# SBUF offsets of matmul operands, and 128-row score passes, in a four-layer trunk kernel

## The chip, the cores and the metric

The kernel runs on one core of one Trainium2 chip. The metric is the device time of one execution in microseconds (us); lower is better. TensorE (PE) does the matmuls, VectorE (DVE), ScalarE (ACT) and GpSimd (POOL) the element-wise work, and DMA queues issued from SyncE (SP) load the weights.

## The reference

A diffusion trunk of four layers over 512 latent tokens and 256 context tokens of 1024 channels. Layer i has a token mixer (0 and 3: gated short convolution; 1: windowed attention with sinks; 2: differential attention) and a gated convolutional FFN of width 2816. All arithmetic is float32.

```python
h = h + gt1 * y                                    # y: the mixer's output
a, g = jnp.split(x @ w_up, 2, axis=-1)             # conv_ffn
return (jax.nn.silu(dwconv(g, conv_w) + conv_b) * a) @ w_down
# layer 1: 16 query heads, 4 KV heads of 64 channels, blocks of 128 query rows
s_lat = jnp.einsum("bqhgd,bkhd->bhgqk", q_j, k_j) * scale    # neighbouring blocks
s_lat = jnp.where(mask, s_lat, -jnp.inf)
s_ctx = jnp.einsum("bqhgd,bkhd->bhgqk", q_j, kc) * scale     # all 256 context keys
p = jax.nn.softmax(jnp.concatenate([s_lat, s_ctx, s_sink], axis=-1), axis=-1)
```

## The kernel before

Float32 accuracy comes from split operands: every value is a high part and a low part in a reduced float32 (fp32r), and a product is three passes, high·high, low·high and high·low (`mm3`, lines 158 to 162; `tok_project`, lines 675 to 677, has its own copy). A weight block arrives by DMA as `wr`, ACT rounds it to `wh` (L108), DVE subtracts to get `wl` (L109). A pass streams a moving operand of 256 or 512 columns against a stationary block of 128 by 128.

Program order: layer 0 convolution (tiles pb, pc, ph, down projection pd), FFN (up projections pg and pa, down projection pd over pairs of its 22 chunks of 128 channels), then layer 1 (`window_gqa`), its FFN, layer 2 (`diff_attn`), its FFN, layer 3. Up projections have normalised activations `xh`, `xl` moving and weights stationary; pd has the mixer's product `mh`, `ml` moving. The first passes of a phase (tile pre) do both halves of a chunk pair. The latent stream is 512 columns wide, or two halves of 256 where phases overlap; the context stream is 256 wide.

Layer 1 first projects tokens (tile pj: K and V, then two groups of queries, each over 6 token tiles and 8 chunks), with weights moving and tokens stationary. `post_kv` normalises and rotates K, splits it into high `ks` (stored twice side by side, 128 rows after the transpose) and low `kl` (64 rows per head, two heads in a tile), transposes both on TensorE (tile pkt) and copies them to `kT1` and `kT2`. `pre` splits four query heads into `qs`, in which high and low part of a head lie side by side, and transposes (tile pqt) to `qT` of 128 rows. A score `psS` of one query head and 128 queries is then three passes for context queries and six or seven for latent ones (`scores`): a two-column pass that writes the sink logit (L789), the latent keys against `kT1` (L792), the masks of the edge blocks (L795), the context keys against `kT1` (L796), and the two low passes against `kT2` (L797 context, L799 latent), which use only the 64 rows of the query's high part. DVE takes the maximum (L801), ACT the exponential (L803), POOL scales by the reciprocal sum (L812). `values` transposes the probabilities (pPT, L828), ACT and DVE split them (L831, L832), and TensorE multiplies with V (pO, L838); the sums go to `m`, `mh`, `ml`, the operands of the out projection, in a rotating set of buffers (L817).

What sets the order: the code makes generators (`scores`, `values`, `prefetch`, down projections as filler), `timeline` interleaves them by a list of due times, and the framework's scheduler then orders each engine's queue, waiting by semaphores where tiles depend on each other or share memory. Tiles come from pools: a pool hands out addresses in the order of its `tile` calls, a tag rotates over `bufs` buffers, and a pool that is opened after another has closed takes over its memory and waits for its readers. So the place of a `tile` call decides the byte offset of that tile and of all behind it.

Of the kernel before, what the change touches and what calls it, by code (L numbers as in the profile page):

```python
# [45 lines left out]
class Trunk:  # L46
# [133 lines left out]
    def setup(self, es):  # L180
        tc, nc, A = self.tc, self.nc, self.A
        self.cp = cp = es.enter_context(tc.tile_pool(name="const", bufs=1))
        self.pp = es.enter_context(tc.tile_pool(name="psum", bufs=1, space=PSUM))
        self.WR, self.WS = 3, 5
        self.wpool = es.enter_context(tc.tile_pool(name="w", bufs=1))
        es.enter_context(tc.tile_pool(name="top", bufs=1, side="right")).tile([P, 8], F32, name="top")

        npk = self.A["pack"].shape[1]
        pk = cp.tile([P, -(-npk // 16) * 16], F32, name="pack")
        nc.sync.dma_start(pk[:, :npk], self.A["pack"])  # L190
        pos = 0
# [12 lines left out]
        nc.scalar.activation(self.cpair, craw, AF.Silu)  # L204
        eye = self.ntmp("eye")[:, :P]
        make_identity(nc, eye)
        self.identr = cp.tile([P, P], F32R, name="identr")
        nc.vector.tensor_copy(self.identr, eye)
        self.ident = self.identr.bitcast(F32)
        self.ones = cp.tile([P, P], F32, name="ones")  # L210
        nc.gpsimd.memset(self.ones, 1.0)
        self.mhalf = cp.tile([P, 16], F32, name="mhalf")
        nc.gpsimd.memset(self.mhalf, -0.5)

        self.ada_b = [take(6, KC) for _ in range(DEPTH)]
        self.g1 = [take(KC) for _ in range(DEPTH)]
        self.g2 = [take(KC) for _ in range(DEPTH)]
        self.fcw = [take(NF, 3) for _ in range(DEPTH)]
        self.fcb = [take(NF) for _ in range(DEPTH)]
        self.scw = {l: take(KC, 3) for l in (0, 3)}  # L220
        self.sink = take(16)
        self.subln = take(1)
        self.mods = {}
        for l in range(DEPTH):
            for s in ((0, 1) if l < 3 else (0,)):
                self.mods[l, s] = cp.tile([P, 6, KC], F32, name=f"mod{l}_{s}")
        hL = [cp.tile([P, SEQ], F32, name=f"hL{k}") for k in range(KC)]
# [14 lines left out]
    def ada_first(self):  # L242

        nc = self.nc
        for j in range(KC):
# [14 lines left out]
            cols = acc[:, 2 * P:].rearrange("p (m v e) -> p m v e", m=2, v=2)[:, :, :, 0]  # L260
            md = self.cp.tile([P, 2, 2], F32, name=f"md{j}", tag="md", bufs=KC)
            nc.vector.tensor_tensor(md, cols, self.ada_b[0][:, 0:2, j:j + 1].to_broadcast([P, 2, 2]), ALU.add)
            gs = self.cp.tile([P, 2], F32, name=f"gs{j}", tag="gs", bufs=KC)
            nc.vector.scalar_tensor_tensor(gs, md[:, 1, :], 1.0, self.g1[0][:, j:j + 1].to_broadcast([P, 2]),
# [234 lines left out]
    def pads(self, y, streams):  # L499
        self.gp = []  # L500
        for i in range(2):
            g = y.tile([P, TOK + 16], F32, name=f"gp{i}")
            for col in (0, SEQ + 1, TOK + 2):
                self.nc.gpsimd.memset(g[:, col:col + 1], 0.0)
            self.gp.append(g)
# [175 lines left out]
    def window_gqa(self, xn):  # L681
# [4 lines left out]
        self.PT, self.rl = 3, 0  # L686
        ytc = self.tc.tile_pool(name="yt1", bufs=1, side=self.yside)
        yt = ytc.__enter__()
        tabs = {which: self.rope_table(1, which, yt) for which in "kq"}
        sink = self.sink  # L690
        sel = y.tile([P, P], F32R, name="sel")
        sinkx = y.tile([P, 32], F32R, name="sinkx")
        pick = self.ntmp("pick")
        nc.gpsimd.memset(pick, 0.0)
        nc.gpsimd.memset(pick[0:1, :P], 1.0)
        nc.gpsimd.memset(pick[32:33, :P], 1.0)
        nc.vector.tensor_copy(sel, pick[:, :P])
        nc.vector.tensor_copy(sinkx, pick[:, P:P + 32])
        nc.vector.tensor_copy(sinkx[0:1, :16], sink[0:1])
        sinkh = self.ntmp("sinkh", F32R)[:, :16]  # L700
        nc.vector.tensor_copy(sinkh, sink)
        nc.vector.tensor_tensor(sinkx[32:33, :16], sink[32:33], sinkh[32:33].bitcast(F32), ALU.subtract)
        identr = self.identr
# [3 lines left out]
        kT1 = {0: y.tile([P, 4, SEQ], F32R, name="kT1L"), 1: y.tile([P, 4, CTX], F32R, name="kT1C")}  # L707
        kT2 = {0: y.tile([P, 2, SEQ], F32R, name="kT2L"), 1: y.tile([P, 2, CTX], F32R, name="kT2C")}
        vs = [y.tile([P, 4, 2, HD], F32R, name=f"v{t}") for t in range(NT)]
        qraw = [y.tile([P, D], F32, name=f"qraw{t}") for t in range(NT)]  # L710

# [3 lines left out]
        def post_kv(tt, ps):  # L715
# [5 lines left out]
            ks = yt.tile([P, 4, 2, HD], F32R, name="ks", tag="pt", bufs=self.PT)  # L721
            kl = yt.tile([P, 512], F32R, name="kl", tag="pt", bufs=self.PT)[:, :256]
            k3 = kr.rearrange("p (h d) -> p h d", d=HD)
            nc.scalar.copy(ks, k3[:, :, None, :].to_broadcast([P, 4, 2, HD]))
            nc.vector.tensor_tensor(kl.rearrange("p (h d) -> p h d", d=HD), k3, ks[:, :, 0, :].bitcast(F32), ALU.subtract)
            pt = self.ps("pkt")
            for j in range(4):
                self.tr(pt[:, j * P:(j + 1) * P], ks[:, j].rearrange("p a d -> p (a d)"))
            for j in range(2):
                self.tr(pt[:, 512 + j * P:512 + (j + 1) * P], kl[:, j * P:(j + 1) * P])  # L730
            sid, o = (0, tt * P) if tt < SEQ // P else (1, tt * P - SEQ)
            nc.scalar.copy(kT1[sid][:, :, o:o + P], pt[:, 0:512].rearrange("p (j t) -> p j t", j=4))
            nc.scalar.copy(kT2[sid][:, :, o:o + P], pt[:, 512:768].rearrange("p (j t) -> p j t", j=2))

        self.wlimit = self.wpos + 12 if PRM['pf1'] else self.wlimit
        tts = [4, 5, 0, 1, 2, 3]
        self.tok_project([A["l1_wa_qkv"][2, kp] for kp in range(4)], xn, tts, post_kv)
        for grp in range(2):
            def post_q(tt, ps, grp=grp):
                self.qk_post(ps, 8, tabs["q"], rope_tt(tt), qraw[tt][:, grp * 512:(grp + 1) * 512], yt)  # L740
            self.tok_project([A["l1_wa_qkv"][grp, kp] for kp in range(4)], xn, tts, post_q)
# [10 lines left out]
        mask = xb.tile([P, 2, P], F32R, name="mask")  # L752
        nc.vector.tensor_copy(mask, maskf)

        def pre(j, tt):
# [18 lines left out]
        def scores(u):  # L774
            _, _, tt, j, _, _ = units[u]
            qT = qTs.pop(u)
            plist = pls[u] = []
            hs = slice((j % 2) * HD, (j % 2) * HD + HD)
            keys, b0, nl = keys_of(tt)
# [5 lines left out]
            for i in range(4):  # L785
# [97 lines left out]
        for _ in self.rest:  # L883
            pass
        self.close_x()
        yc.__exit__(None, None, None)
        self.xside = self.yside
# [10 lines left out]
    def diff_attn(self, xn):  # L898
# [7 lines left out]
        vsp = dr.__enter__().tile([2, 8, P, NT, P], F32R, name="vspill")  # L906
        nlam = y.tile([P, 16], F32, name="nlam")[:, :1]
        kT = [y.tile([P, 8, TOK], F32R, name=f"kT{grp}") for grp in range(2)]
# [137 lines left out]
        def finish(st):  # L1046
# [258 lines left out]
```

## Time and profile before

| what | value |
|---|---|
| median of 3 runs | 3202.27 us (3201.17 to 3203.89) |
| the profiled execution, its own time | 3210.95 us |
| span of its trace | 3209.1 us |
| mean granted TensorE clock | 0.981 |
| PE busy (share of span) | 3136.9 us (98%) |
| PE weight loads | 2717.5 us (85%) |
| DVE busy | 2177.0 us (68%) |
| ACT busy | 1126.4 us (35%) |
| POOL busy | 698.7 us (22%) |
| DMA moved | 322.66 MB, mean 101 GB/s |

Busy time is the union of an engine's records. A matmul's record is modelled at its end and reaches into the next one, so the busy share of PE says little; the start times of successive records are what can be compared. [...] The profiled execution is 0.27% above the median of the runs.

### The profile page before, as it was taken

The numbers are of one execution on the slowest core, as the hardware profiler recorded it, in microseconds if no ns is written. First come the engines' busy times: TensorE is split into PE (matmuls) and PEld (weight loads), VectorE is DVE, ScalarE is ACT, GpSimd is POOL, SyncE is SP. The second block draws the span as 40 slices with busy tenths as digits, with TensorE's granted clock in tenths as the row PEclk, the third lists the DMA queues.
The fourth block names the chain that finished last, engine by engine and source line by source line (L and its number), as shares of the span: only waits on it lengthen the run. The fifth ranks groups of instructions, "written<-read, shape, count | busy, mean of one in ns | idle before, by whom it ended". The sixth has DMA issues, their size and how long they took to land.

```text
span 3209.1 us, 44079 instructions
## 1 busy us (share of the span) xinstructions
PE 3136.9 (98%) x17548; PEld 2717.5 (85%) x17548; DVE 2177.0 (68%) x3138; ACT 1126.4 (35%) x1864; POOL 698.7 (22%) x581
## 2 busy tenths in 40 slices
PE   8999999999998999999999999989999999999999
PEld 7889888888987788888888888778888888898888
DVE  5775887786575566677666576478788766565555
ACT  4212322222243566422222244277532333242222
POOL 2222221231134333122000033277211110010000
PEclk9999999999998799899999999999999999999999
DMA  6431434332111000233333212421255522222322
GB/s 227 145 119 53 138 126 144 132 119 99 47 62 34 20 1 27 87 115 104 128 109 130 78 48 70 135 73 57 91 196 164 200 98 99 99 86 88 104 91 79
DMA packets 105198, 322.66 MB, mean 101 GB/s; under 512 B 12576, under 2 KB 27552, under 8 KB 104992
## 3 DMA queue, kind: packets, MB, share of 16 engines
q1 hardware_dynamic: 100512, 313.26, 28.6%
q0 software_dynamic: 4480, 6.58, 1.1%
q8 instruction: 138, 2.26, 0.3%
q14 instruction: 68, 0.56, 0.1%
HBM read 311.26 MB, written 8.53 MB: 100 GB/s over the span
## 4 chain that ended last, share of the span: by engine, by line
PE 90%; DVE 5%; ACT 2%; issue 1%; DMA 1%; POOL 1%; SPq 0%; DVEq 0%; ACTq 0%; POOLq 0%
PE pd L160 9%; PE pd L161 9%; PE pd L162 9%; PE pg L160 6%; PE pg L162 6%; PE pg L161 6%; PE pa L160 6%; PE pa L161 6%; PE pa L162 6%; PE pj L675 3%; PE pj L676 3%; PE pj L677 3%; PE pO L838 2%; PE pPT L828 1%; PE pre L161 1%; PE pre L162 1%
## 5 line engine op out<-in xcount | busy, mean ns | idle before, releaser
L108 ACT CAST wh<-wr 128x1024 fp32r<-128x1024 f32 x380 | 392.9, 1049 | 1211.2 <-PE pd L161 357.2
L109 DVE TENSOR_TENSOR wl<-wr,wh 128x1024 fp32r<-128x1024 f32 x380 | 485.5, 1291 | 175.5 <-ACT wh L108 173.3
L160 PE MATMUL pd<-mh,wh 128*128 128x256 f32 (+1 forms) x1712 | 566.3, 331 | 10.7 <-DVE hC L435 10.2
L161 PE MATMUL pd<-ml,wh 128*128 128x256 f32 (+1 forms) x1712 | 562.0, 328 | 0.3 <-DVE ml L1069 0.3
L162 PE MATMUL pd<-mh,wl 128*128 128x256 f32 (+1 forms) x1712 | 562.2, 328 | 0.0
L435 DVE SCALAR_TENSOR_TENSOR hL<-pd,mod,hL 128x512 f32<-128x512 f32 (+1 forms) x512 | 333.9, 659 | 257.7 <-PE pd L162 257.1
L294 POOL PARTITION_ALL_REDUCE acc<-acc x34 | 222.8, 6584 | 1103.7 <-DVE acc L292 1103.7
L160 PEld LDWEIGHTS pd<-mh,wh 128*128 128x128 f32 x1712 | 324.5, 190 | 44.0 <-DVE hC L435 10.6
L160 PE MATMUL pg<-xh,wh 128*128 128x256 f32 (+1 forms) x992 | 352.3, 355 | 1.5 <-ACT gp L580 1.5
L162 PE MATMUL pg<-xh,wl 128*128 128x256 f32 (+1 forms) x992 | 352.1, 355 | 0.0
L161 PE MATMUL pg<-xl,wh 128*128 128x256 f32 (+1 forms) x992 | 351.9, 355 | 0.0
L161 PE MATMUL pa<-xl,wh 128*128 128x256 f32 (+1 forms) x992 | 351.5, 354 | 0.0
L160 PE MATMUL pa<-xh,wh 128*128 128x256 f32 (+1 forms) x992 | 351.4, 354 | 0.0
L162 PE MATMUL pa<-xh,wl 128*128 128x256 f32 (+1 forms) x992 | 351.0, 354 | 0.0
L161 PEld LDWEIGHTS pd<-ml,wh 128*128 128x128 f32 x1712 | 324.4, 190 | 31.1 <-DVE ml L1069 0.5
L162 PEld LDWEIGHTS pd<-mh,wl 128*128 128x128 f32 x1712 | 324.8, 190 | 30.5
L292 DVE SCALAR_TENSOR_TENSOR acc<-adaw,csilu,acc 128x1024 f32<-128x1024 f32 x238 | 300.9, 1293 | 57.7 <-DMA adaw<-l_ada_w 56.9
L160 PEld LDWEIGHTS pg<-xh,wh 128*128 128x128 f32 x992 | 187.5, 189 | 28.4 <-ACT gp L580 1.7
L162 PEld LDWEIGHTS pg<-xh,wl 128*128 128x128 f32 x992 | 187.4, 189 | 27.0
L161 PEld LDWEIGHTS pg<-xl,wh 128*128 128x128 f32 x992 | 187.2, 189 | 26.8
L162 PEld LDWEIGHTS pa<-xh,wl 128*128 128x128 f32 x992 | 187.0, 189 | 27.0
L160 PEld LDWEIGHTS pa<-xh,wh 128*128 128x128 f32 x992 | 187.1, 189 | 26.9
(239 smaller groups left out, 5778.8 us busy)
## 6 DMA issues: line engine op xcount, KB each, us to landing
adaw<-l_ada_w SPq DMA_DIRECT2D x176, 512.0 KB, 4.2
wr<-l_ffn_up SPq DMA_DIRECT2D x176, 512.0 KB, 4.1
wr<-l_ffn_down SPq DMA_DIRECT2D x88, 512.0 KB, 3.5
wr<-l_sc_in SPq DMA_DIRECT2D x48, 512.0 KB, 3.7
wr<-l_da_qkv SPq DMA_DIRECT2D x24, 512.0 KB, 3.9
adaf<-l_ada_first SPq DMA_DIRECT2D x16, 512.0 KB, 6.0
wr<-l_sc_out SPq DMA_DIRECT2D x16, 512.0 KB, 3.6
wr<-l_wa_qkv SPq DMA_DIRECT2D x12, 512.0 KB, 3.8
```

The lines of the kernel that those rows point to most:

```text
L108: keep(self.nc.scalar.copy(hi, raw))
L109: keep(self.nc.vector.tensor_tensor(lo, raw, hi.bitcast(F32), ALU.subtract))
L160: mm(ps, wh, xh, start=first, stop=False)
L161: mm(ps, wh, xl, start=False, stop=False)
L162: mm(ps, wl, xh, start=False, stop=last)
L292: keep(nc.vector.scalar_tensor_tensor(acc[v], raw, c, acc[v], ALU.mult, ALU.add))
L294: nc.gpsimd.partition_all_reduce(acc[v], acc[v], P, bass.bass_isa.ReduceOp.add)
L435: nc.vector.scalar_tensor_tensor(hk, ps, gate[sid][:, oc:oc + 1], hk, ALU.mult, ALU.add)
L675: mm(o, xh, wh[:, w], start=k == 0, stop=False)
L676: mm(o, xl, wh[:, w], start=False, stop=False)
L677: mm(o, xh, wl[:, w], start=False, stop=k == KC - 1)
L838: nc.tensor.matmul(po, vw, t, start=n == 1 and i == 0, stop=n == len(keys) and i == 1)
```

## The change

Three things change.

First, tiles that meet in a matmul get equal byte offsets modulo 256 within an SBUF partition. Padding tiles are added (`pad0`, `pad1`, `ypad`, `xpad`), some tiles grow (`top`, `pack`, `nlam`, `sinkx`), some shrink or move to another pool (`ones`, `md`, `gs`, the query gain), and in layer 1 the order of pools changes: the K and V tiles come before the temporaries, the raw queries `qraw` get a pool of their own that opens after the K part's temporaries close, and `sel` and `sinkx` are made behind the mask, in the pool of the scores. The pair `mh`, `ml` of the layer-1 out projection has two buffers in place of three, and the two-operand sum of squares in layer 2 (oss) uses a `ones` of two columns.

Second, `kl` is written twice side by side as `ks` was, four transposes per token tile in place of two bring it to 128 rows per head, and `kT2` has four heads of 128 rows in place of two of two heads each.

Third, with that the low passes of a score use all 128 rows of `qT`. They add the product of the query's low part with the key's low part, which was left out before.

The offsets modulo 256 of moving and stationary operand, from the addresses of the two compiled programs:

| passes | before | after |
|---|---|---|
| pre, pb, pc, ph, pg, pa of layers 0, 2, 3 | 64 and 64 | 0 and 0 |
| pre, pg, pa of layer 1's FFN | 192 and 64 | 0 and 0 |
| pd of layers 0, 2, 3 (mixer and FFN) | 192 and 64 | 0 and 0 |
| pd of layer 1: out projection | 64 and 64 | 0 and 0 |
| pd of layer 1: FFN | 128 and 64 | 0 and 0 |
| pj of layer 1 | 64 and 64 | 0 and 0 |
| pj of layer 2 | 64 and 192 | 0 and 0 |
| layer 1: psS from kT1, kT2 | 192 and 192 | 0 and 128 |
| layer 1: pO | 128 and 192 | 0 and 0 |
| layer 2: psS | 128 and 192 | 0 and 0 |
| layer 2: pO | 192 and 192 | 0 and 0 |

The core of the diff:

```diff
-        es.enter_context(tc.tile_pool(name="top", bufs=1, side="right")).tile([P, 8], F32, name="top")
+        es.enter_context(tc.tile_pool(name="top", bufs=1, side="right")).tile([P, 56], F32, name="top")
...
-        pk = cp.tile([P, -(-npk // 16) * 16], F32, name="pack")
+        cp.tile([P, PADS[0]], F32, name="pad0")
+        pk = cp.tile([P, -(-npk // 64) * 64 + 16], F32, name="pack")
...
-        self.ones = cp.tile([P, P], F32, name="ones")
+        self.ones = cp.tile([P, 2], F32, name="ones")
...
+        cp.tile([P, PADS[1]], F32, name="pad1")
...
+        y.tile([P, 48], F32, name="ypad")
...
-        kT2 = {0: y.tile([P, 2, SEQ], F32R, name="kT2L"), 1: y.tile([P, 2, CTX], F32R, name="kT2C")}
+        kT2 = {0: y.tile([P, 4, SEQ], F32R, name="kT2L"), 1: y.tile([P, 4, CTX], F32R, name="kT2C")}
         vs = [y.tile([P, 4, 2, HD], F32R, name=f"v{t}") for t in range(NT)]
-        qraw = [y.tile([P, D], F32, name=f"qraw{t}") for t in range(NT)]
+        ytc = self.tc.tile_pool(name="yt1", bufs=1, side=self.yside)
+        yt = ytc.__enter__()
...
-            kl = yt.tile([P, 512], F32R, name="kl", tag="pt", bufs=self.PT)[:, :256]
+            kl = yt.tile([P, 4, 2, HD], F32R, name="kl", tag="pt", bufs=self.PT)
+            k4 = kr.rearrange("p (h d) -> p h d", d=HD)[:, :, None, :].to_broadcast([P, 4, 2, HD])
+            nc.scalar.copy(ks, k4)
+            nc.vector.tensor_tensor(kl, k4, ks.bitcast(F32), ALU.subtract)
...
-            for j in range(2):
-                self.tr(pt[:, 512 + j * P:512 + (j + 1) * P], kl[:, j * P:(j + 1) * P])
+            for j in range(4):
+                self.tr(pt[:, 512 + j * P:512 + (j + 1) * P], kl[:, j].rearrange("p a d -> p (a d)"))
...
-            nc.scalar.copy(kT2[sid][:, :, o:o + P], pt[:, 512:768].rearrange("p (j t) -> p j t", j=2))
+            nc.scalar.copy(kT2[sid][:, :, o:o + P], pt[:, 512:1024].rearrange("p (j t) -> p j t", j=4))
...
+        ytc.__exit__(None, None, None)
+        yqc = self.tc.tile_pool(name="yq1", bufs=1, side=self.yside)
+        yq = yqc.__enter__()
+        qraw = [yq.tile([P, D], F32, name=f"qraw{t}") for t in range(NT)]
+        ytc = self.tc.tile_pool(name="yt1q", bufs=1, side=self.yside)
+        ytq = ytc.__enter__()
...
+        sel = xb.tile([P, P], F32R, name="sel")
+        sinkx = xb.tile([P, 64], F32R, name="sinkx")
+        pick = self.ntmp("pick")
+        nc.gpsimd.memset(pick, 0.0)
+        nc.gpsimd.memset(pick[0:1, :P], 1.0)
+        nc.gpsimd.memset(pick[32:33, :P], 1.0)
...
+        xb.tile([P, XPAD], F32, name="xpad")
...
-                mm(oc, qT[hs, i, :], kT2[1][hs, j // 2, :], start=False, stop=True)
+                mm(oc, qT[:, i, :], kT2[1][:, j, :], start=False, stop=True)
                 if nl:
-                    mm(ol, qT[hs, i, :], kT2[0][hs, j // 2, b0 * P:b0 * P + nl], start=False, stop=True)
+                    mm(ol, qT[:, i, :], kT2[0][:, j, b0 * P:b0 * P + nl], start=False, stop=True)
...
-                mids[s] = [mp.tile([P, 4, 256], F32R, name=f"m{x}", tag=f"m{x}", bufs=3) for x in "hl"]
+                mids[s] = [mp.tile([P, 4, 256], F32R, name=f"m{x}", tag=f"m{x}", bufs=2) for x in "hl"]
...
-                nc.tensor.matmul(pss[:, t * P:(t + 1) * P], sq[:, t * P:(t + 1) * P], self.ones, start=True, stop=True)
+                nc.tensor.matmul(pss[:, t * P:t * P + 2], sq[:, t * P:(t + 1) * P], self.ones, start=True, stop=True)
```

Most of the order stays. It moves where layer 1 hands over from the projections to the scores. On TensorE the kernel before has there, in a row (names: pj token projection, sinkx the sink logits, pqt query transposes):

```order
L677 MATMUL pj<-wl_8493,xh_7_7939 128x512
L789 MATMUL psS<-sinkx,sel 128x2 x2
L165 MATMUL pqt<-identr,qs 128x128 x4
L792 MATMUL psS<-kT1L,qT 128x256 x2
L165 MATMUL pqt<-identr,qs 128x128 x4
L795 MATMUL psS<-mask,identr 128x128
L796 MATMUL psS<-kT1C,qT 128x256
L797 MATMUL psS<-kT2C,qT 128x256
L799 MATMUL psS<-kT2L,qT 128x256
```

and the changed kernel:

```order
L685 MATMUL pj<-wl_8503,xh_7_7942 128x512
L167 MATMUL pqt<-identr,qs 128x128 x8
L804 MATMUL psS<-sinkx,sel 128x2
L807 MATMUL psS<-kT1L,qT 128x256
L804 MATMUL psS<-sinkx,sel 128x2
L807 MATMUL psS<-kT1L,qT 128x256
L810 MATMUL psS<-mask,identr 128x128
L811 MATMUL psS<-kT1C,qT 128x256
L812 MATMUL psS<-kT2C,qT 128x256
L814 MATMUL psS<-kT2L,qT 128x256
```

The two sink passes have moved behind both sets of query transposes, because the sink tile is now made late. The low passes (L797 and L799, now L812 and L814) keep their place and columns; the rows that a pass uses do not show in this listing.

On POOL, at the same place, the kernel before:

```order
L659 TENSOR_TENSOR qraw_8118<-pu,pw 128x512
L171 TENSOR_TENSOR rstd<-qss,mhalf 128x8
L659 TENSOR_TENSOR qraw_8119<-pu,pw 128x512
L748 MEMSET maskf 128x256
L750 AFFINE_SELECT maskf<-maskf 128x128 x2
```

and the changed kernel:

```order
L667 TENSOR_TENSOR qraw_8475<-pu,pw 128x512
L173 TENSOR_TENSOR rstd<-qss,mhalf 128x8
L760 MEMSET pick 128x512
L761 MEMSET pick 1x128
L762 MEMSET pick 1x128
L667 TENSOR_TENSOR qraw_8476<-pu,pw 128x512
L751 MEMSET maskf 128x256
L753 AFFINE_SELECT maskf<-maskf 128x128 x2
```

Three fills of `pick` now stand ahead of the last raw query tile. DVE turns them into `sel` and `sinkx` in the changed kernel, in four steps ahead of the mask:

```order
L158 TENSOR_TENSOR qs<-qraw_8473,qs 128x4x64
L763 CAST sel<-pick 128x128
L764 CAST sinkx<-pick 128x64
L765 CAST sinkx<-pack 1x16
L768 TENSOR_TENSOR sinkx<-pack,sinkh 1x16
L756 CAST mask<-maskf 128x256
L158 TENSOR_TENSOR qs<-qraw_8474,qs 128x4x64
```

where the kernel before has the mask (L753) directly behind the query split (L156).

## Rows read from the trace of the kernel before

**Rows 1.** The page, the chain that ended last, by engine.

```profile
PE 90%; DVE 5%; ACT 2%; issue 1%; DMA 1%; POOL 1%; SPq 0%; DVEq 0%; ACTq 0%; POOLq 0%
```

**Rows 2.** Windows, PE, tile pa: window, length, busy (count), clock, DMA share, GB/s.

```profile
355.28:363.62 8.34, 8.34 (x48) 1.00 0.66 208
1345.70:1354.13 8.43, 8.43 (x48) 1.00 0.55 190
2946.14:2951.58 5.44, 5.44 (x24) 1.00 0.28 96
```

**Rows 3.** Windows, PE, tile pd.

```profile
1282.94:1292.88 9.94, 9.94 (x83) 1.00 0.01 2
1849.03:1864.53 15.50, 15.50 (x131) 1.00 0.10 35
2951.58:2956.70 5.12, 5.12 (x22) 1.00 0.22 59
3182.29:3204.96 22.67, 22.67 (x189) 1.00 0.19 71
```

**Rows 4.** Windows, PE, tile pj, layer 1 and layer 2.

```profile
949.73:997.17 47.44, 47.44 (x209) 1.00 0.10 34
1915.62:1922.89 7.27, 7.27 (x31) 1.00 0.04 11
```

**Rows 5.** Timeline of PE, a latent score: start, duration, operation, operands, partitions x columns.

```profile
1110.30 0.33 PE L796 MATMUL psS<-kT1C,qT 128*128 128x256 f32 x1
1110.56 0.38 PE L797 MATMUL psS<-kT2C,qT 64*128 64x256 f32 x1
1110.78 0.33 PE L799 MATMUL psS<-kT2L,qT 64*128 64x384 f32 x1
1111.05 1.09 PE L828 MATMUL pPT<-identr,pP 128*128 128x128 f32 x8
...
1113.41 0.39 PE L160 MATMUL pd<-mh,wh 128*128 128x256 f32 x1
1113.64 0.28 PE L161 MATMUL pd<-ml,wh 128*128 128x256 f32 x1
```

**Rows 6.** Timeline of PE, a context score.

```profile
1090.23 0.36 PE L796 MATMUL psS<-kT1C,qT 128*128 128x256 f32 x1
1090.53 0.38 PE L797 MATMUL psS<-kT2C,qT 64*128 64x256 f32 x1
1090.84 0.39 PE L160 MATMUL pd<-mh,wh 128*128 128x256 f32 x1
```

**Rows 7.** Groups of PE by form, whole span: count, busy us, mean ns, idle before.

```profile
L160 PE MATMUL pd<-mh,wh 128*128 128x512 f32 x688 | 272.4, 396 | 0.0
L675 PE MATMUL pj<-wh,xh 128*128 128x512 f32 x400 | 159.1, 398 | 5.5 <-DVE pt L643 5.4
```

**Rows 8.** Groups of PE by form, 1337 to 1895 us, FFN of layer 1.

```profile
L160 PE MATMUL pd<-mh,wh 128*128 128x256 f32 x240 | 67.7, 282 | 5.1 <-DVE hC L435 5.1
...
L162 PE MATMUL pg<-xh,wl 128*128 128x512 f32 x168 | 66.4, 395 | 0.0
...
L160 PE MATMUL pd<-mh,wh 128*128 128x512 f32 x144 | 57.1, 397 | 0.0
```

**Rows 9.** Groups of PE by form, 1080 to 1290 us.

```profile
L797 PE MATMUL psS<-kT2C,qT 64*128 64x256 f32 x69 | 26.7, 386 | 0.0
```

**Rows 10.** Windows: length, busy of PE, PEld, DVE, ACT, POOL (counts), clock, DMA.

```profile
1003.00:1030.00 27.00, 25.57 (x92) 20.09 (x92) 12.11 (x20) 12.71 (x29) 7.53 (x12) 0.51 0.06 20
1080.00:1186.00 106.00, 104.81 (x676) 87.94 (x676) 66.17 (x128) 67.54 (x162) 39.73 (x55) 0.98 0.00 1
2090.00:2290.00 200.00, 183.56 (x1251) 164.35 (x1251) 155.51 (x265) 139.41 (x295) 134.82 (x133) 0.98 0.17 54
```

**Rows 11.** Timeline of PE, the hand-over to the scores of layer 1.

```profile
1002.02 0.68 PE L165 MATMUL pqt<-identr,qs 128*128 128x128 f32 x4 [4.34 <-DVE qs L156]
```

**Rows 12.** Groups of POOL by form, 990 to 1045 us.

```profile
L748 POOL MEMSET maskf<- 128x256 f32 x1 | 0.3, 316 | 0.1
```

More of the change, by code (lines that the diff above doesn't have):

```diff
@@ L20 @@
 EARLY = (4, 5)
+PADS = (32, 56)
+XPAD = 48
 D = 1024
@@ L260, in ada_first @@
             cols = acc[:, 2 * P:].rearrange("p (m v e) -> p m v e", m=2, v=2)[:, :, :, 0]
-            md = self.cp.tile([P, 2, 2], F32, name=f"md{j}", tag="md", bufs=KC)
+            md = self.first.tile([P, 2, 2], F32, name=f"md{j}", tag="md", bufs=KC)
             nc.vector.tensor_tensor(md, cols, self.ada_b[0][:, 0:2, j:j + 1].to_broadcast([P, 2, 2]), ALU.add)
-            gs = self.cp.tile([P, 2], F32, name=f"gs{j}", tag="gs", bufs=KC)
+            gs = self.first.tile([P, 2], F32, name=f"gs{j}", tag="gs", bufs=KC)
             nc.vector.scalar_tensor_tensor(gs, md[:, 1, :], 1.0, self.g1[0][:, j:j + 1].to_broadcast([P, 2]),
@@ L616, in rope_table @@
         nc, A = self.nc, self.A
-        g = yt.tile([P, 2, HD], F32, name=f"gain{l}{which}")
+        if which == "q":
+            g = self.cp.tile([P, 2, HD], F32, name=f"gain{l}q", tag="n1", bufs=3)
+        else:
+            g = yt.tile([P, 2, HD], F32, name=f"gain{l}k")
         nc.sync.dma_start(g, A[f"l{l}_gain"][:, "qk".index(which)])
@@ L686, in window_gqa @@
         self.PT, self.rl = 3, 0
-        ytc = self.tc.tile_pool(name="yt1", bufs=1, side=self.yside)
-        yt = ytc.__enter__()
-        tabs = {which: self.rope_table(1, which, yt) for which in "kq"}
+        tabs = {}
         sink = self.sink
[L691 to L702, printed above, removed]
         identr = self.identr
@@ L707, in window_gqa @@
         kT1 = {0: y.tile([P, 4, SEQ], F32R, name="kT1L"), 1: y.tile([P, 4, CTX], F32R, name="kT1C")}
-        kT2 = {0: y.tile([P, 2, SEQ], F32R, name="kT2L"), 1: y.tile([P, 2, CTX], F32R, name="kT2C")}
+        kT2 = {0: y.tile([P, 4, SEQ], F32R, name="kT2L"), 1: y.tile([P, 4, CTX], F32R, name="kT2C")}
         vs = [y.tile([P, 4, 2, HD], F32R, name=f"v{t}") for t in range(NT)]
-        qraw = [y.tile([P, D], F32, name=f"qraw{t}") for t in range(NT)]
+        ytc = self.tc.tile_pool(name="yt1", bufs=1, side=self.yside)
+        yt = ytc.__enter__()
+        for which in "kq":
+            tabs[which] = self.rope_table(1, which, yt)
         def rope_tt(tt):
@@ L721, in post_kv @@
             ks = yt.tile([P, 4, 2, HD], F32R, name="ks", tag="pt", bufs=self.PT)
-            kl = yt.tile([P, 512], F32R, name="kl", tag="pt", bufs=self.PT)[:, :256]
-            k3 = kr.rearrange("p (h d) -> p h d", d=HD)
-            nc.scalar.copy(ks, k3[:, :, None, :].to_broadcast([P, 4, 2, HD]))
-            nc.vector.tensor_tensor(kl.rearrange("p (h d) -> p h d", d=HD), k3, ks[:, :, 0, :].bitcast(F32), ALU.subtract)
+            kl = yt.tile([P, 4, 2, HD], F32R, name="kl", tag="pt", bufs=self.PT)
+            k4 = kr.rearrange("p (h d) -> p h d", d=HD)[:, :, None, :].to_broadcast([P, 4, 2, HD])
+            nc.scalar.copy(ks, k4)
+            nc.vector.tensor_tensor(kl, k4, ks.bitcast(F32), ALU.subtract)
             pt = self.ps("pkt")
@@ L737, in window_gqa @@
         self.tok_project([A["l1_wa_qkv"][2, kp] for kp in range(4)], xn, tts, post_kv)
+        ytc.__exit__(None, None, None)
[4 more added lines that the diff above has]
+        ytq = ytc.__enter__()
         for grp in range(2):
             def post_q(tt, ps, grp=grp):
-                self.qk_post(ps, 8, tabs["q"], rope_tt(tt), qraw[tt][:, grp * 512:(grp + 1) * 512], yt)
+                self.qk_post(ps, 8, tabs["q"], rope_tt(tt), qraw[tt][:, grp * 512:(grp + 1) * 512], ytq)
             self.tok_project([A["l1_wa_qkv"][grp, kp] for kp in range(4)], xn, tts, post_q)
@@ L753, in window_gqa @@
         nc.vector.tensor_copy(mask, maskf)
+        sel = xb.tile([P, P], F32R, name="sel")
[4 more added lines that the diff above has]
+        nc.gpsimd.memset(pick[32:33, :P], 1.0)
+        nc.vector.tensor_copy(sel, pick[:, :P])
+        nc.vector.tensor_copy(sinkx, pick[:, P:P + 64])
+        nc.vector.tensor_copy(sinkx[0:1, :16], sink[0:1])
+        sinkh = self.ntmp("sinkh", F32R)[:, :16]
+        nc.vector.tensor_copy(sinkh, sink)
+        nc.vector.tensor_tensor(sinkx[32:33, :16], sink[32:33], sinkh[32:33].bitcast(F32), ALU.subtract)
+        xb.tile([P, XPAD], F32, name="xpad")
         def pre(j, tt):
@@ L777, in scores @@
             plist = pls[u] = []
-            hs = slice((j % 2) * HD, (j % 2) * HD + HD)
             keys, b0, nl = keys_of(tt)
@@ L885, in window_gqa @@
         self.close_x()
+        yqc.__exit__(None, None, None)
         yc.__exit__(None, None, None)
@@ L906, in diff_attn @@
         vsp = dr.__enter__().tile([2, 8, P, NT, P], F32R, name="vspill")
-        nlam = y.tile([P, 16], F32, name="nlam")[:, :1]
+        nlam = y.tile([P, 64], F32, name="nlam")[:, :1]
         kT = [y.tile([P, 8, TOK], F32R, name=f"kT{grp}") for grp in range(2)]
```

## The prediction

> **What bounds the kernel now.** I read the chain of waits first: TensorE work makes up 90% of it, everything else 10% [rows 1]. So whatever the change does to helpers counts only where TensorE waits for them, and the question is how long a TensorE pass takes. A matmul's recorded duration is modelled and overlaps its successor's, so I never use it. In a stretch of back-to-back passes of one tile, the time from start to start is the window divided by its count.
>
> Read that way, the two groups of FFN operands differ. The 24 up-projection passes of layer 3 take 5.44 us, 226.7 ns each; both their operands sit at offset 64 modulo 256. The 22 down-projection passes right behind them, same engine, same full clock, same 512 columns, take 5.12 us, 232.7 ns each; their operands are 128 bytes apart [rows 2, 3]. The token projections repeat it: 209 passes of layer 1 (64 and 64) at 227.0 ns, 31 of layer 2 (64 and 192) at 234.5 ns [rows 4]. So disagreement costs 6.0 to 7.5 ns per 512-column pass. With 256 columns it costs nothing: 119.8 ns where they agree, 120.0 ns where they are 128 bytes apart, and 118.3 ns where they are 64 apart [rows 3].
>
> The other half is the low K pass of the scores. In a latent score the full-row context pass starts at 1110.30, the 64-row pass behind it only at 1110.56: 0.26 us for 256 columns, against 0.12 us for such a pass among its equals [rows 3, 5]. The next gap, between two 64-row passes, is 0.22 us, again 0.10 too long; the 384-column 64-row pass then takes 0.27 us, where 384 columns lie between 120 and 227 ns, about 0.17 us; and behind the return to 128 rows the first pass takes 0.23 us instead of 0.12 [rows 5]. A context score shows 0.30 and 0.31 us in place of 0.12 [rows 6]. No wait is shown at any of these gaps.
>
> **The change part by part.**
>
> *A. Agreement.* Passes that come to agree, each times its price: (1) the 512-column down projections outside the FFN of layer 1: 688 per line less 144, three lines, 1632 passes [rows 7, 8] at 6.0 ns, 9.8 us. (2) The layer-2 token projections: 400 per line less 144 in layer 1 (3 groups, 6 token tiles, 8 chunks), so 256 times 3, 768 passes [rows 7] at 7.5 ns, 5.8 us. (3) The FFN of layer 1, up: a block of 24 narrow and 24 wide passes takes 8.43 us against 8.34 us in layer 0 where operands agree [rows 2], which is 3.75 ns per wide pass; 168 in each of six groups [rows 8], 1008 passes, 3.8 us. (4) Its down projections are 64 apart: 432 wide passes [rows 8], unpriced in these rows, between 0 and 6.0 ns; at 3 ns 1.3 us; and 720 narrow ones that lose 1.5 ns each [rows 3], 1.1 us back. (5) Layer-2 scores and the values passes of layer 1, about 300 wide passes at 0 to 6 ns, 0.9 us. Sum 20.5 us if all lay on the chain. A tenth of the chain is not TensorE [rows 1], so I take **18 us**. [...]
>
> One thing is not covered by any row: offset 0 itself. All wide agreeing passes measured sit at 64. Between 0 and 64 I expect no difference; if the gap between operands is not what counts, the term falls, and a rival below holds that.
>
> *B. Scores with 128 rows.* The doubled half adds products of two low parts, no columns and no pass: 96 context passes and 64 latent ones (16 heads times 6 and times 4 token tiles) keep their shapes. What goes is the gaps. Latent score: 0.14 + 0.10 + 0.10, plus 0.11 behind it [rows 5]: 0.45 us. Context score: 0.18 + 0.19 [rows 6], plus 0.1 behind it as there: 0.47 us. For 64 and 32 scores that is 44 us of TensorE, or 34 us without the passes behind; from below nothing, if the gap belongs to the change of weights' tile and not to the rows.
>
> What of it becomes time? Between 1080 and 1290 us 69 of the 96 scores run [rows 9], 31 us of gap. There TensorE is now idle 1% only, with ACT and DVE busy 64% and 62% [rows 10]. Without the gaps the same helper work falls into some 180 us, at 72 to 74%, which is the load of the layer-2 attention between 2090 and 2290 us (ACT 70%, DVE 78%), where TensorE is idle 8% [rows 10]. So 208 − 31 = 177 us of TensorE work fits into 192 us, and 18 of 31 us are saved. [...] Together **28 us**, with 0 and 44 as ends.
>
> [...]
>
> *C. What it adds.* Twelve more transposes; eight back to back take 1.09 us with the last one's tail [rows 5], so at most 0.14 us each, 1.6 us. The ACT copy of the doubled part and the DVE subtraction twice as wide: hidden behind token projections, 24 passes or 5.4 us per tile [rows 4]. qraw now opens after the K tables' pool closes and so waits for the last K tile, but the token projection's PSUM is read before that and no pass waits. At the hand-over to the scores TensorE already idles 4.34 us for the first query split [rows 11]. Three fills of pick now stand on POOL ahead of the last qraw; by the nearest fill (0.3 us, [rows 12]) 0.6 to 0.9 us, and four small DVE steps stand ahead of the mask: on the path, 1 us at most, 0 if the mask's own wait hides them. Two-column oss passes: nothing, as the weight load stays. Two out-projection buffers instead of three: nothing, because the last pass reading a pair stands tens of passes ahead of the next write into it; if that cover is gone it is the slow rival. C costs **2 us**.
>
> Sum: −18 − 28 + 2 = −44 us on 3210.95 us, which is 3167. That profiled run was 8.7 us above the median of 3202.27, so against the runs: **3158 us**.
>
> **The rivals.** (i) *Rows gain nothing in time*, chance 0.15: the gaps close but TensorE waits for exp, POOL's scaling or the clock instead, or they stay because they come with the change from one K tile to the next and not with the 64 rows. For: no row shows a full-row pass in that place. Against: TensorE idles 1% there now, and full-row passes of other tiles follow each other at 0.12. [...] −18 + 2: **3186 us**. (ii) *Agreement gains nothing*, 0.07: it was something else about those tiles, or offset 0 differs. [...] −28 + 2: **3176 us**. (iii) *The whole gap is saved*, 0.10: the helpers keep up and denser work lifts the clock earlier. −18 − 45 + 2: **3141 us**. (iv) *Neither*, 0.05: the tiles do not land as meant, or both effects were misread: **3204 us**. (v) *Slower*, 0.03: with two m buffers ACT stands at the mh copy until an out-projection block has been read. A block of 96 narrow passes is 11.5 us at 120 ns [rows 3]; exp and the copies of the transposed probabilities queue behind it on ACT, TensorE empties, and a restart at 0.51 clock for 27 us loses another 13. Four re-uses exist, 24.7 us each; two cancel the gain, three give 3158 + 74 = **3232 us**. Against it: the order puts those reads well ahead.
>
> **How the numbers follow.** Forecast 0.60, then 0.15, 0.07, 0.10, 0.05 and 0.03. Its own range is 3143 to 3173. The range 3140 to 3186 takes in (ii), (iii) and half of (i); outside lie half of (i), (iv), (v) and a tail of (iii), under 0.2. A measurement of this kernel can tell 0.2%, 6.4 us, from no change. Faster: the forecast, (i), (ii) and (iii), 0.92; same: (iv), 0.05; slower: (v), 0.03.
>
> **What would show it.** Down-projection windows of 512 columns at 227 ns and layer-2 token projections too; latent scores whose passes follow at 0.12 and 0.17 us; TensorE's idle time rising to some 8% between first and last score. Wide passes still at 232 would break A, gaps of 0.2 us between score passes B, and idle time of TensorE on mh or ml would mean (v).

## The result, and the profile after

The changed kernel takes 3159.6 us (median of 4 runs, 3157.1 to 3163.3) against 3203.1 us of the kernel before; the ratio is 0.986, 95% interval 0.9848 to 0.9872. That is 43.5 us less; 44 were forecast, and 3158 us. Each of the three terms behind that sum was off, though, and they cancelled. The experiments below measure them one by one.

The chain of waits is what it was, TensorE nine tenths [rows 1]:

```profile
PE 90%; DVE 5%; ACT 2%; issue 1%; DMA 1%; POOL 1%; SPq 0%; ACTq 0%; DVEq 0%; POOLq 0%
```

Windows of back-to-back passes of the down projection (tile pd) in the changed kernel, columns as in [rows 2]:

```profile
1801.62:1817.46 15.84, 15.84 (x132) 1.00 0.10 34
2934.73:2939.72 4.99, 4.99 (x22) 1.00 0.14 47
3130.38:3153.04 22.66, 22.66 (x189) 1.00 0.18 71
```

and of the token projection (tile pj) of layer 2:

```profile
1868.40:1875.46 7.06, 7.06 (x32) 1.00 0.07 12
```

The 22 wide down projections now take 226.8 ns each where 232.7 stood [rows 3]; the token projections of layer 2 come down from 234.5 [rows 4] to 227.7 ns (the 32 counted include one that reaches into the window, so the time is shared by 31). Narrow passes stay at 120 ns, and those of layer 1's FFN rise from 118.3 ns at 64 bytes [rows 3] to 120.0.

Not every down projection followed. Six wide ones in a row in layer 0, in the kernel before and then in the changed kernel (233.2 and 231.2 ns each by their start times):

```profile
503.78:505.18 1.40, 1.40 (x6) 1.00 0.00 0
```

```profile
501.45:502.84 1.39, 1.39 (x6) 1.00 0.05 21
```

Over all wide down projections at full clock the mean from start to start goes from 232.4 to 231.0 ns in layer 0 and from 230.9 to 230.4 in layer 1's FFN, but from 232.7 to 227.7 in layer 2 and from 233.0 to 226.7 in layer 3. By the table of offsets all four agree in the changed kernel; why only two of them reach 227 ns was not found.

The timeline of PE, a latent score with 384 latent keys:

```profile
1084.07 0.33 PE L811 MATMUL psS<-kT1C,qT 128*128 128x256 f32 x1
1084.24 0.28 PE L812 MATMUL psS<-kT2C,qT 128*128 128x256 f32 x1
1084.36 0.34 PE L814 MATMUL psS<-kT2L,qT 128*128 128x384 f32 x1
...
1088.63 0.34 PE L814 MATMUL psS<-kT2L,qT 128*128 128x384 f32 x1
1088.80 1.03 PE L843 MATMUL pPT<-identr,pP 128*128 128x128 f32 x8
```

The steps are 0.17, 0.12 and 0.17 us where 0.26, 0.22 and 0.27 stood [rows 5]: the second and third are what the prediction named, the first keeps 0.05 us over a narrow pass.

Where did the time go? The stretch from the last token projection of layer 1 to the first pass of its FFN, as a window (length, busy time of PE, PEld, DVE, ACT and POOL with counts, clock, DMA share, GB/s). The kernel before, in the profiled execution of the prediction:

```profile
997.40:1298.33 300.93, 285.71 (x1669) 236.48 (x1667) 182.51 (x323) 180.16 (x402) 109.77 (x137) 0.88 0.05 17
```

the changed kernel, that stretch, and the part of it from 1060 us:

```profile
996.97:1254.76 257.79, 236.38 (x1670) 214.89 (x1669) 180.15 (x328) 178.81 (x402) 111.89 (x139) 0.95 0.06 19
1060.00:1250.00 190.00, 184.35 (x1385) 170.06 (x1383) 135.60 (x245) 135.42 (x302) 81.28 (x102) 1.00 0.04 12
```

So 43 us of the 52 us between these two executions lie in the score stage. Not all of that is the change, as experiment 11 shows.

### The profile page after: what moved, and what is told of

Its sections match the earlier page's. It is cut to its first block, busy times and chain, and to the rows that moved or that the text cites. A ratio compares the mean times of both kernels' runs of the same rounds, so it can differ in the third digit from the quotient of the medians.

```text
span 3157.2 us, 44102 instructions
## 1 busy us (share of the span) xinstructions
PE 3083.3 (98%) x17560; PEld 2706.2 (86%) x17560; DVE 2175.6 (69%) x3138; ACT 1126.7 (36%) x1864; POOL 695.9 (22%) x581
## 4 chain that ended last, share of the span: by engine, by line
PE 90%; DVE 5%; ACT 2%; issue 1%; DMA 1%; POOL 1%; SPq 0%; ACTq 0%; DVEq 0%; POOLq 0%
PE pd L162 9%; PE pd L163 9%; PE pd L164 9%; PE pg L162 6%; PE pg L163 6%; PE pg L164 6%; PE pa L163 6%; PE pa L162 6%; PE pa L164 6%; PE pj L683 3%; PE pj L684 3%; PE pj L685 3%; PE pre L163 1%; PE pre L164 1%; PE pre L162 1%; PE pb L162 1%
## 5 line engine op out<-in xcount | busy, mean ns | idle before, releaser
L162 PE MATMUL pd<-mh,wh 128*128 128x256 f32 (+1 forms) x1712 | 563.4, 330 | 10.5 <-DVE hC L439 10.3
```

What stands on the lines that cost most here:

```text
L162: mm(ps, wh, xh, start=first, stop=False)
```

## The experiments

Times are medians; the kernel before, in the runs beside each group, had 3204 to 3205 us. The changed kernel was timed in the first group alone, beside 3203.1 us, so a difference to it can be off by some 2 us.

**1. The low passes back on 64 rows.** The changed kernel with

```diff
-                mm(oc, qT[:, i, :], kT2[1][:, j, :], start=False, stop=True)
+                mm(oc, qT[hs, i, :], kT2[1][hs, j, :], start=False, stop=True)
...
-                    mm(ol, qT[:, i, :], kT2[0][:, j, b0 * P:b0 * P + nl], start=False, stop=True)
+                    mm(ol, qT[hs, i, :], kT2[0][hs, j, b0 * P:b0 * P + nl], start=False, stop=True)
```

> The changed kernel with one edit: both low passes of a score again use the 64 rows of the query's high part (of the doubled K tile; layout and all else as changed). Theory P (the prediction's sizes: rows 28 us, agreement 18 us): 3160 + 28 = 3188 us. Theory Q (read from the two traces: the score stage of layer 1 became 43 us shorter and all the rest 10 us, so rows 40 us, agreement 9 us): 3200 us. Rival (the gaps belong to the change of K tile, not to the rows): 3160 us, gaps between score passes unchanged at 0.17 and 0.12 us. P and Q both expect 0.26 us in front of the context low pass and 0.22 us in front of the latent one.

Measured: 3195.4 us (6 runs, 3194.7 to 3196.2), so the rows are worth 35.8 us, between P and Q; the third reading falls. The timeline of PE in this kernel:

```profile
1111.84 0.33 PE L812 MATMUL psS<-kT1C,qT 128*128 128x256 f32 x1
1112.10 0.38 PE L813 MATMUL psS<-kT2C,qT 64*128 64x256 f32 x1
1112.32 0.28 PE L815 MATMUL psS<-kT2L,qT 64*128 64x256 f32 x1
1112.53 0.66 PE L844 MATMUL pPT<-identr,pP 128*128 128x128 f32 x4
```

Same tiles, same addresses, same order, only the rows differ, and the steps of 0.26 and 0.22 us are back. The whole difference lies in the score stage, which takes 36 us more than the 257.79 us of the changed kernel, at a lower granted clock (0.92 for 0.95):

```profile
995.37:1289.14 293.77, 276.90 (x1669) 229.96 (x1668) 182.52 (x328) 179.93 (x402) 113.44 (x139) 0.92 0.05 17
```

**2. The old disagreements back.** The changed kernel with

```diff
-        es.enter_context(tc.tile_pool(name="top", bufs=1, side="right")).tile([P, 56], F32, name="top")
+        es.enter_context(tc.tile_pool(name="top", bufs=1, side="right")).tile([P, 24], F32, name="top")
```

> The changed kernel with one constant: the tile top has 24 columns in place of 56, which shifts all pools on the right side of SBUF by 128 bytes and so restores, nearly pass for pass, the disagreements that the kernel before had (1632 wide down projections, 768 token projections of layer 2, 1008 wide up projections of layer 1's FFN). Theory P: 9.8 + 5.8 + 3.8 = 19.4 us of passes, nine tenths of it on the chain: 3177 us. Theory Q: half of that arrives, 3169 us. [...]

Measured: 3174.0 us (4 runs, 3172.0 to 3175.0): agreement is worth 14.4 us, again between P and Q. Tile pd of the last FFN:

```profile
2915.66:2920.78 5.12, 5.12 (x22) 1.00 0.18 50
```

That is 232.7 ns, the value of [rows 3], from one constant in a pool that no matmul reads.

**3. All weights 128 bytes off.** The changed kernel with 32 columns of padding ahead of the weight pool and 32 behind:

```diff
+        es.enter_context(tc.tile_pool(name="wpad0", bufs=1)).tile([P, 32], F32, name="wpad0")
         self.wpool = es.enter_context(tc.tile_pool(name="w", bufs=1))
+        es.enter_context(tc.tile_pool(name="wpad1", bufs=1)).tile([P, 32], F32, name="wpad1")
```

> The changed kernel with the weight pool alone shifted by 128 bytes (and the rest shifted back), so that all 8208 wide passes of up, down and token projections are 128 bytes apart. Theory P: 8208 times 6 ns is 49 us, nine tenths on the chain, 3204 us. Theory Q: half, 3182 us. [...] In the trace P and Q expect some 233 ns a wide pass and still 120 ns a narrow one.

Measured: 3194.4 us (6 runs, 3192.9 to 3197.5), 34.8 us more than the changed kernel. Windows of tile pa (wide) and tile pd (narrow):

```profile
2893.59:2899.16 5.57, 5.57 (x24) 1.00 0.28 94
```

```profile
3166.64:3188.00 21.36, 21.36 (x180) 1.00 0.17 65
```

232.1 ns and 118.7 ns. Over all wide passes at full clock the mean from start to start is 232.6 ns against 227.8 in the changed kernel, over all narrow ones 118.8 against 119.5. So 8208 times 4.8 less 6624 times 0.7 is 39.4 − 4.6 = 34.8 us: the measured loss, with nothing taken off for the chain. P's price per pass was too high and its tenth off was wrong. On agreement this is the plainest run: only addresses moved, and 35 us came.

**4. Agreement at another offset.** The changed kernel with everything moved to 64:

```diff
-PADS = (32, 56)
+PADS = (32, 72)
...
-        es.enter_context(tc.tile_pool(name="top", bufs=1, side="right")).tile([P, 56], F32, name="top")
+        es.enter_context(tc.tile_pool(name="top", bufs=1, side="right")).tile([P, 40], F32, name="top")
```

> The changed kernel with all operands of those passes at offset 64 in place of 0, still agreeing. If only the distance of the two operands counts (P and Q): 3160 us within 5. If offset 0 itself is worth something, or 64 is, it moves by more than that, some 8 us for each ns a wide pass.

Measured: 3157.2 us (4 runs, 3155.0 to 3159.2). Whether the operands agree at 0 or at 64 makes no difference that these runs can tell, which the prediction had left uncovered.

**5. Both undone.** Edits 1 and 2 together:

> The changed kernel with both edits taken back at once: low passes on 64 rows, and the right side of SBUF shifted so that the old disagreements stand. What is left of the change is its by-work: doubled K tile, 12 more transposes, later sink tiles, two out-projection buffers, two-column ones. If the two parts add up: 3160 + 36 + 14 = 3210 us, which is 5 us above the kernel before, and these 5 us are the price of the by-work (the prediction said 2). If they overlap (passes made shorter where TensorE waits anyway): at or below the kernel before, 3200 to 3205 us.

Measured: 3210.4 us (12 runs, 3206.8 to 3219.0), 1.0019 of the kernel before (1.0009 to 1.0028). The parts add up (3209.8 was the sum), so the by-work costs about 6 us (3 to 9 by the interval). Start times place some of it: the token projections of layer 1, from first to last pass, take 104.0 us in place of 102.9 (the 12 transposes), and in layer 1's FFN 720 narrow passes lost 1.5 ns each, 1.1 us. The hand-over to the scores, in the changed kernel's timeline of PE:

```profile
1004.63 0.75 PE L167 MATMUL pqt<-identr,qs 128*128 128x128 f32 x4 [2.43 <-DVE qs L158]
1005.46 0.34 PE L804 MATMUL psS<-sinkx,sel 128*128 128x2 f32 x1
...
1007.01 0.52 PE L811 MATMUL psS<-kT1C,qT 128*128 128x256 f32 x1
```

The first context pass starts 10.3 us behind the last token projection's start (996.74); before it was 9.1 us. That is 1.2 us. The rest, some 3 us, is no larger than the doubt on the 6 and was not traced to an edit; part of it lies behind the scores of layer 2, where the stretch up to the FFN takes 36.0 us in place of 35.1 (35.9 to 36.4 in the changed kernel and all its variants).

**6. Only the context pass on 64 rows.** The first line of edit 1 alone.

> The changed kernel with only the context low pass of each score on 64 rows, the latent low pass on 128. If each 64-row pass costs by itself, wherever it stands: 96 of 160 passes, 36 * 96 / 160 = 21 us, 3181 us. If the cost belongs to entering and leaving the 64-row state (two changes per score, however many passes lie between): nearly all of the 36 us, 3190 us or more. Gaps: 0.26 us in front of the context pass in both; behind it 0.22 us by both, so the time and the step in front of the pass after the latent one (0.17 against 0.27 us) tell.

Measured: 3194.1 us (5 runs, 3192.6 to 3199.4): 34.5 of the 35.8 us are back with 96 of 160 passes. So the cost goes by the score and not by the pass: it belongs to entering and leaving the 64 rows. The timeline of PE:

```profile
1111.80 0.33 PE L812 MATMUL psS<-kT1C,qT 128*128 128x256 f32 x1
1112.06 0.38 PE L813 MATMUL psS<-kT2C,qT 64*128 64x256 f32 x1
1112.37 0.39 PE L815 MATMUL psS<-kT2L,qT 128*128 128x256 f32 x1
1112.60 0.82 PE L844 MATMUL pPT<-identr,pP 128*128 128x128 f32 x6
```

and the weight loads (PEld) of the same passes:

```profile
1111.74 0.19 PEld L812 LDWEIGHTS psS<-kT1C,qT 128*128 128x128 f32 x1
1112.06 0.18 PEld L813 LDWEIGHTS psS<-kT2C,qT 64*128 64x128 f32 x1
1112.37 0.19 PEld L815 LDWEIGHTS psS<-kT2L,qT 128*128 128x128 f32 x1
```

Beside them the weight loads of the changed kernel, for the score shown in the section on the result (passes at 1084.07, 1084.24 and 1084.36):

```profile
1084.01 0.19 PEld L811 LDWEIGHTS psS<-kT1C,qT 128*128 128x128 f32 x1
1084.12 0.19 PEld L812 LDWEIGHTS psS<-kT2C,qT 128*128 128x128 f32 x1
1084.24 0.19 PEld L814 LDWEIGHTS psS<-kT2L,qT 128*128 128x128 f32 x1
```

and those of the two 64-row passes of run 1 (passes at 1112.10 and 1112.32):

```profile
1112.10 0.18 PEld L813 LDWEIGHTS psS<-kT2C,qT 64*128 64x128 f32 x1
1112.21 0.19 PEld L815 LDWEIGHTS psS<-kT2L,qT 64*128 64x128 f32 x1
```

Among full rows the load for a low pass starts 0.12 us ahead of it, beside the pass before. From one 64-row pass to the next it is ahead too, by 0.11 us. Where the rows change, it starts with the pass (1112.06 and 1112.37 here, 1112.10 in run 1): nothing hides it, on the way in and on the way out. The step behind the isolated 64-row pass is 0.31 us, the one before it 0.26 and the one after 0.23. Over all such scores at full clock the medians are 264, 311 and (for 384 columns) 282 ns against 173, 120 and 175: 0.39 us for a short visit, as for a visit of two passes (263, 225, 265 and 223 ns in run 1 against 173, 119, 175 and 117).

**7. Weights 192 bytes off.** As 3, with 48 columns ahead and 16 behind.

> The changed kernel with the weight pool shifted by 192 bytes: 7008 wide passes stand 64 apart (moving above stationary), 1200 token projections 192 apart, 6600 narrow passes 64 apart. From start-to-start means of the kernel before (512 columns: 227.6 agreeing, 230.7 at 64, 235 to 238 at 192; 256 columns: 119.4 agreeing, 117.6 at 64): 7008 * 3.1 + 1200 * 8 - 6600 * 1.8 = 22 + 10 - 12 = 20 us, 3180 us. If 64 apart cost as much as 128 apart: 3195 us as with that shift. If narrow passes were indifferent: 3191 us.

Measured: 3153.4 us (4 runs, 3150.5 to 3157.2), faster than the changed kernel. All three expectations missed. Tile pa, narrow and wide:

```profile
349.77:352.49 2.72, 2.72 (x25) 1.00 0.32 86
2882.46:2887.96 5.50, 5.50 (x24) 1.00 0.77 268
```

24 narrow passes (one more reaches in) take 113.3 ns each, where the changed kernel needs 119.6; wide ones 229.2, against 226.7. The means over all passes are 115.8 against 119.5 and 229.0 against 227.8. With them 6600 * 3.7 − 7008 * 1.2 − 1200 * 6.5 = 24.4 − 8.4 − 7.8 gives 8 us gained; 6.2 were measured.

**8. Context tiles 64 off, meant as a better version.**

```diff
+            apart = sid and (second or l % 3 == 0)
+            if apart:
+                xp.tile([P, 16], F32, name="xpad0")
             self.xn_next[whole] = [[xp.tile([P, whole[1]], F32R, name=f"x{x}{sid}_{k}", tag=f"x{x}{sid}", bufs=KC)
                                     for x in "hl"] for k in range(KC)]
+            if apart:
+                xp.tile([P, 48], F32, name="xpad1")
```

> A version meant to beat the changed kernel: as changed, but the context tiles of the normalised activations, which only narrow passes of the convolutions and FFNs read, lie 64 bytes off the weights (16 columns of padding in front, 48 behind). 2688 narrow passes at 117.6 in place of 119.5 ns: -5 us, 3155 us. If narrow passes gain nothing from 64, or the gain is lost where TensorE waits for operands: 3160 us.

Measured: 3154.6 us (4 runs, 3150.7 to 3156.7), as expected, though the intervals of the two ratios touch (0.9826 to 0.9852 here, 0.9848 to 0.9872 for the changed kernel); tile pa, narrow, 117.9 ns:

```profile
353.12:355.95 2.83, 2.83 (x24) 1.00 0.37 97
```

**9. Both ideas mixed.** The changed kernel with

```diff
-PADS = (32, 56)
+PADS = (32, 40)
...
+            gap = 48 if l == 2 and not second else 16 if l == 0 and sid else 0
+            if gap:
+                xp.tile([P, gap], F32, name=f"xpa{sid}")
...
+            if gap:
+                xp.tile([P, 64 - gap], F32, name=f"xpb{sid}")
...
-        y.tile([P, 48], F32, name="ypad")
+        y.tile([P, 64], F32, name="ypad")
```

where the two ifs enclose the normalised tiles as in 8.

> A version meant to beat the changed kernel, by the prices measured so far: all left-side pools, the weights among them, moved to offset 192 by a smaller padding tile, and three paddings more, so that wide up and token projections agree where they can, while 5280 narrow passes stand 64 apart from weights at 192 (from start to start 115.8 in place of 119.5 ns in the kernel with the weights at 192). 5280 narrow passes gain 3.7 ns, 19.5 us; 3072 wide passes 64 apart lose 1.2 ns, 3.7 us; 304 wide passes of layers 1 and 2 at 192 apart lose 6 ns, 2 us: 3160 - 14 = 3146 us. If narrow passes gain only the 1.5 ns that the padded context tiles gained (weights at 0): 3158 us.

Measured: 3149.7 us (5 runs, 3146.7 to 3154.9), 0.9827 of the kernel before (0.981 to 0.9843), the lowest median of this study, though run 7's interval (0.9819 to 0.9848) overlaps. 10 of the 14 us came: the narrow mean is 116.5 ns, not 115.8, and the wide mean at 64 apart 229.7, not 229.0. Tile pa, narrow, 64 apart from weights at 192 as in run 7, but 117.9 ns and not 113.3:

```profile
350.45:353.28 2.83, 2.83 (x24) 1.00 0.37 114
```

**10. Only the low weights 128 off.** 32 columns ahead of the low weight tiles inside the weight pool, 32 behind the pool.

```diff
+        if i == 0:
+            self.wpool.tile([P, 32], F32, name="wlpad")
         lo = self.wpool.tile([P, D], F32R, name=f"wl{i}", tag="wl", bufs=self.WS)
```

> The changed kernel with the low weight tiles alone shifted by 128 bytes. In an up projection the passes go: high x with high w, low x with high w, high x with low w. If a pass is slowed by the distance between its moving operand and its own weights, the third (line with high x, low w) takes 232 ns and the others 227. If it is slowed by the distance between its moving operand and the weights that are loaded for the next pass meanwhile, the second (low x, high w) takes 232 and the others 227. Time in both: a third of the 35 us of the kernel with all weights shifted, some 3171 us.

Measured: 3186.1 us (one run), 26.5 us above the changed kernel, not 11. The timeline of PE, tile pa:

```profile
2909.76 0.39 PE L164 MATMUL pa<-xh,wh 128*128 128x512 f32 x1
2909.98 0.40 PE L165 MATMUL pa<-xl,wh 128*128 128x512 f32 x1
2910.22 0.40 PE L166 MATMUL pa<-xh,wl 128*128 128x512 f32 x1
2910.45 0.39 PE L164 MATMUL pa<-xh,wh 128*128 128x512 f32 x1
2910.68 0.40 PE L165 MATMUL pa<-xl,wh 128*128 128x512 f32 x1
```

From start to start 0.22, 0.24, 0.23, 0.23 us. Over all of pa at full clock the means are 227.4 for the first pass, 232.3 for the second and 234.0 for the third, so both expectations hold half: the distance to the weights that are being loaded and that to the own weights both show. It does not stop there: in the token projections even the second of three passes (high weights moving, low tokens, all at 0) takes some 234 ns. Which of the distances count was not settled.

**11. The kernel before again, for its profile.**

> The kernel before, once more, for its profile: the profiled execution that the prediction used was 8.7 us above the median of its runs. If that lay in one stage (the first scores, with their clock): the span between the last token projection of layer 1 and its FFN, 301 us there, is some 7 us shorter here, near the 294 us of the changed kernel with 64-row passes. If it is spread evenly: 300 us.

Measured: 3201.5 us (one run), and the score stage:

```profile
995.75:1288.53 292.78, 277.23 (x1669) 230.21 (x1668) 180.89 (x323) 179.75 (x402) 110.83 (x136) 0.92 0.05 17
```

8.2 us shorter than in the first profile, with no other stage more than 2 us apart: the surplus that the prediction subtracted at the end sat there. The granted clock is 0.92 for 0.88. The clock records of the traces hold two levels, 1.0 and 0.5 (the kernel before has a granted 0.50 from 1060 to 1065 us), and with them that is some 47 us of this stage at 0.5 in place of 72 (twice what the clock lacks to 1, times the length), so the two executions of one kernel differ in how long TensorE stood at the lower level behind its idle time at the start (4.34 us, [rows 11]).

## Why the prediction was right

**What bounds it** held. Start-to-start steps read from windows were the right measure, and both kinds of gap vanished in the windows that were named: the down projections of layer 3, the token projections of layer 2, the scores. The down projections of layer 0 and of layer 1's FFN hardly moved.

**A, agreement: 18 forecast, 14.4 measured (run 2).** Two steps failed against each other. The price was read from a few undisturbed windows (6.0 and 7.5 ns, [rows 3, 4]); the mean over all wide passes is 4.8 ns (run 3). What was lost by it can be placed: the 528 down projections of layer 0 were given 6.0 ns each, 3.2 us, and gained 1.4, 0.7 us; the token projections of layer 2 were given 7.5 ns and gained 5.4 (means of 232.8 and 227.4). And a tenth was taken off because a tenth of the chain is not TensorE; run 3 shows the whole sum arriving. A likely reason, not tested, is that these passes stand in stages where TensorE hardly waits.

**B, rows: 28 forecast, 35.8 measured (run 1).** Against run 1, where only the rows differ, TensorE's busy time in the score stage falls from 276.9 to 236.4 us, by 40.5. That looks like the 44 us of gaps that were forecast, but part of it is a shorter stay at the lower clock, for which the forecast had no term (it stands in rival (iii)): the records of the clock put 50 us of the stage at the 0.5 level in run 1 and 27 in the changed kernel (granted clock 0.92 and 0.95). A 256-column pass of a score takes 0.21 us there and 0.12 at the full level (213 and 120 ns from start to start, the medians of the low context pass in the changed kernel), so 23 us less are worth at most half, 11 us by this estimate, and the gaps themselves 29 us or more; at 0.39 us for each of 96 scores (run 6) they would be 37. The gaps were sized somewhat high, then, and the shorter stay at the lower level made up for it. It is no accident of one execution: 27 to 35 us in the eight traced kernels with 128 rows throughout, 42 to 73 in the five traces with 64-row passes. Of the 28 us, 10 stood for the 27 scores at the start of the stage, and no run shows that term by itself: from the last token projection to the context pass of the 28th score the trace of the kernel before takes 83.1 us and that of the changed kernel 66.9, 16 us less, with 58 and 27 us of them at the 0.5 level. The step that failed is what becomes of the gaps. I had let TensorE's idle time between 1080 and 1290 us rise from 1% to 8%, as in the layer-2 attention [rows 10]. It rose to 3% (184.35 of 190 us from 1060 us on), although ACT and DVE are there at 71%, near the 72 to 74% foreseen. Idle time over the whole stage went from 16.9 to 21.4 us: 40.5 less 4.5 is the 36 us that the stage lost. The waits of PE in the stage show how little came in. Columns: waiting line, releaser, us in total, times, longest. With 64 rows (run 1):

```profile
PE pqt L167 <- DVE qs L158: 7.2, 3, 4.5
PE psS L805 <- ACT pP L819: 2.7, 4, 1.3
PE pPT L844 <- POOL pP L828: 2.4, 3, 1.3
```

the changed kernel:

```profile
PE pqt L167 <- DVE qs L158: 7.6, 3, 4.5
PE psS L804 <- ACT pP L818: 5.0, 7, 1.5
PE pPT L843 <- POOL pP L827: 3.0, 4, 1.3
```

Exp and POOL's scaling are the next things to be late, as rival (i) had it, but with 3 us. A stage's load alone did not tell its idle time: the layer-2 attention, at much the same shares, idles 8%.

**C, by-work: 2 forecast, 6.2 measured (run 5).** The transposes (1.1) and the hand-over (1.2) came close to their prices (1.6 and at most 1); the narrow passes of layer 1's FFN (1.1) had been counted under A. The two-column sums (oss) cost nothing, as said: from start to start a pass takes 112 ns (median) with 128 columns before and with two after, and its weight load 192 ns in both. Some 3 us were not foreseen; with an interval of 3 to 9 us on the whole term they are hardly shown, and no edit was found for them.

The sum: −14.4 − 35.8 + 6.2 = −44.0. Errors of +4, −8 and +4 cancelled, so the exact total is luck where the terms are concerned; the range, made from their bounds, was not.

**The rivals.** (i) fell with run 1, (ii) with runs 2 and 3 (14.4 and 34.8 us). (iii) came half true: 35.8 us on the rows lie midway between the forecast's 28 and its 45, and the clock did rise earlier, as it had it (27 us at the 0.5 level in place of run 1's 50). (iv) fell with the result. (v): no row of PE waits for mh or ml in the score stage of the changed kernel, and ACT waits 1.0 us in all in front of the copy to mh, for DVE and not for an out projection, so two buffers are enough; a kernel with three was not run.

## What to carry to other kernels

Read pass times as steps from start to start, grouped by where the operands lie: a few ns over thousands of passes are worth a padding constant (4.8 ns on each of 8208 wide passes were 39 us in run 3), and the address of a tile is set by every tile allocated before it. Keep the rows of successive passes the same: duplicate a half operand rather than visit 64 rows, since a visit cost 0.39 us here, for one pass as for two. And price a term by the mean of all its passes, not by its cleanest window, before anything is taken off for cover.

## What the runs showed that was not expected

The cost of few rows shows in the weight loads: that of a low pass starts 0.11 to 0.12 us ahead of it behind a pass of the same rows, and only with its pass where the rows change (runs 1 and 6). Why it starts so late there no run shows.

Agreement modulo 256 is not the best placement for every width. Wide passes want it (226.7 ns; 229 at 64 apart with weights at 192, run 7; 232 to 233 at 128 apart, runs 2 and 3). Narrow ones are quicker 64 apart, and by how much differs between kernels with the same distance: 117.9 ns in runs 8 and 9, 113.3 in some blocks of run 7. Nor do all wide ones gain: in the changed kernel the down projections take 231 ns in layer 0 and 227 in layer 3, with the same offsets. Distance modulo 256 is thus not all that counts, and run 10 says the same of its partner: moving the weights of one pass in three cost three quarters of what moving all of them did.
